# Hybrid diffusion block on one core: fixed order for TensorE alone in gate/up and down, first weights split during the last out-projection tile, down weights loaded in fours

## The chip, the cores and the metric

The kernel runs on one core of a Trainium2 chip. The metric is device time in microseconds of one execution. Of the kernel before, three runs are at hand, 3139.68 to 3141.82 us with a median of 3141.06, and one profiled execution.

## The reference

One transformer-like layer over 2048 latent tokens of width 1024, with a context of 256 tokens. Two head groups (gated linear attention and differential attention) read the same modulated input; this study is about what follows them:

```
mix = concatenate([gla_merge(...), diff_merge(...)], axis=-1) @ w_out[l]
x = x + gt1 * mix
x = x + gt2 * swiglu(modulate(x, norm2_g[l], sh2, sc2), w_ffn_in[l], w_ffn_out[l])

def swiglu(h, w_in, w_out):
    gate, up = jnp.split(h @ w_in, 2, axis=-1)
    return (jax.nn.silu(gate) * up) @ w_out
```

The hidden width is 2816, all arrays are float32.

## The kernel before

Each float32 operand is split into a high and a low part (`split`, L89: a copy to the rounded type on ScalarE at L90, the difference on VectorE at L87), and each product is three matmuls (`mm3`, L93 to L96: high by high, high by low, low by high).

**Order.** Under `tc.manual_schedule(engines=...)` the engines named keep the order in which the kernel writes their instructions. The other engines' order is set when the program is built: a planner goes by modelled times, and of the instructions that it holds ready on an engine it takes the one written first. On the chip every engine runs its instructions in the order so planned. `MS` (L41) names TensorE alone; `MS5` (L42) names TensorE, VectorE (DVE) and ScalarE (ACT). SyncE's DMA queue is never named. The attention and out-projection stages use `MS`, gate/up and down use `MS5` (L1215, L1271).

**Out projection (L910 to L1079).** 16 token tiles from 15 down to 0. `prep` (L971) gates and normalises a tile's mixed heads and transposes them; `main` (L1008) multiplies by the eight split blocks of `w_out` (two column halves, eight row blocks, 48 matmuls), and adds into `x1`. The raw `w_out` blocks are loaded at L932 during and after the attention, into buffers of later tokens (`s4x0`, `s4x1`), of the norm (`s4n`) and of the split mix (`s4h`). For each pair of tiles but the last, `mod2` (L1023) squares (L1029), scales (L1031, on ScalarE), transposes (L1044) and modulates (L1047) them, and either stores the result to DRAM (`h2_d`, L1050) or leaves it in `hb`, four blocks of 4 x 512 tokens (tags hb00 to hb11), for the half of the tokens that comes first in gate/up. `early_ops` prepares two of the seven block operands, slots 0 and 1.

**Gate/up (L1082 to L1249).** A seven-product scheme (after Strassen) for 2 x 2 blocks: gate and up as columns, two halves of the 1024 input rows. A round `n` is one block `j` of 128 hidden columns for one half of the tokens; there are 22 rounds per half, 44 in all. Each round has seven products `i` of twelve matmuls, weights against the token operand `slots[i]` (tiles o0h, o0l to o6h, o6l; 128x2048). `rebuild(hb, i)` (L1092) makes slot `i` from the blocks, with a block sum for i = 1, 4, 5; it runs in round 0 for slots 2 to 6 and in round 21, behind each product, for all slots of the other token half. `fetch` (L1134) loads a round's raw weights (tile wi, two DMAs of 512 KB), `weights(n, i)` (L1141) splits the i-th weight combination into a pair of buffers (wh, wl; seven pairs), with three sums at i = 1 and one at i = 6. It is written `AHEAD` = 3 products before its product. Round 22 uses the weights of round 21 again. `finish` (L1184) evicts each product: e on VectorE (L1195 and others, by the helper's L84) or ScalarE (L1187, L1191, L1202). A later product of a round adds into a bank that `finish` of an earlier one must have read. `last_group` (L1104) normalises tiles 0 and 1 in round 1: loads, ScalarE squares, scaling on VectorE (L1115), transposes (L1122).

**Down (L1251 to L1306).** 16 pairs of token tiles (8 pairs for each half of the 1024 output columns). A pair takes 22 hidden blocks x 2 tiles x 3 = 132 matmuls. `down_weights(dd, j)` (L1259) loads one raw block (128x512, 256 KB, tile wo, three buffers), and splits it into wot. `tokens` (L1209) loads and splits half a tile's activations (tile ar, 704 KB). In pair 0 all 22 blocks are loaded and split; those of the second column half follow in pairs 5 and 7. The pools of this stage open when those of gate/up have closed.

Of the kernel before, what the change touches and what calls it, by code (L numbers as in the profile page):

```python
# [11 lines left out]
F32 = mybir.dt.float32  # L12
# [7 lines left out]
P = 128  # L20
# [15 lines left out]
AHEAD = 3  # L36
# [5 lines left out]
MS5 = {mybir.EngineType.PE, mybir.EngineType.DVE, mybir.EngineType.Activation}  # L42
# [10 lines left out]
def dit_block(ctx: ExitStack, tc: tile.TileContext, x, c, cx, c_ctx, w_mod, b_mod, norm1_g, w_in, gate_up,  # L53
# [32 lines left out]
    def sub(o, a, b, eng=None):  # L86
        (eng or V).tensor_tensor(out=o, in0=a, in1=b, op=ALU.subtract)  # L87

    def split(hi, lo, src):  # L89
        S.activation(hi, src, AF.Copy)  # L90
        sub(lo, src, f(hi))
# [804 lines left out]
    with ExitStack() as st:  # L896
        h2p = st.enter_context(tc.tile_pool(name="s45h", bufs=1, reuse_waits="tile"))
        pad = st.enter_context(tc.tile_pool(name="s45pad", bufs=1, side="right"))
        G.memset(pad.tile([P, 56], F32, name="pad"), 0.0)
        rsk = st.enter_context(ExitStack())  # L900
        st6 = st.enter_context(ExitStack())
        sl0 = st6.enter_context(tc.tile_pool(name="s45o", bufs=1, reuse_waits="tile"))
# [4 lines left out]
        def slot(pool, i):  # L907
            return [pool.tile([P, 4, 512], F32R, name=f"o{i}{u}", tag=f"o{i}{u}") for u in "hl"]

        hb = h2_blocks()  # L910
        slots = {i: slot(sl0, i) for i in range(2)}
        st1 = st.enter_context(ExitStack())
        xp = [st1.enter_context(tc.tile_pool(name=f"s4x{u}", bufs=2, side="right", reuse_waits="tile")) for u in range(2)]
        xnp = st1.enter_context(tc.tile_pool(name="s4n", bufs=2, side="right", reuse_waits="tile"))
# [4 lines left out]
        pp = st1.enter_context(tc.tile_pool(name="s4p", bufs=2, reuse_waits="tile"))  # L919
        gl = st1.enter_context(tc.tile_pool(name="s4g", bufs=2, reuse_waits="tile"))  # L920
        wk = st1.enter_context(tc.tile_pool(name="s4k", bufs=2, reuse_waits="tile"))
        ps_gm = st1.enter_context(tc.tile_pool(name="s4gm", bufs=1, space=PSUM, reuse_waits="tile"))
        ps_tp = st1.enter_context(tc.tile_pool(name="s4tp", bufs=3, space=PSUM, reuse_waits="tile"))
        ps_mm = st1.enter_context(tc.tile_pool(name="s4mm", bufs=4, space=PSUM, reuse_waits="tile"))
        gt1 = gp.tile([P, D], F32, name="gt1")
# [3 lines left out]
        for n, k in enumerate(ORD0):  # L929
            pool, tag = {3: (xnp, "xn"), 2: (xnp, "xn"), 1: (ph, "mh"), 0: (ph, "ml")}.get(k, (xp[k // 2 % 2], "xt"))  # L930
            w = pool.tile([P, D], F32, name="wr", tag=tag)
            load(w, w_out[0, k * P:(k + 1) * P, :])  # L932
            with tc.high_priority(offset=tc.cur_priority - marks[3 + 2 * n]):
                split(*wo[k], w)

        def gla_out(lt, mixt):
# [22 lines left out]
            sq = gl.tile([P, 4, P], F32, name="at", tag="at", bufs=1)  # L959
# [11 lines left out]
        def prep(lt):  # L971
# [3 lines left out]
            xt = xp[lt // 2 % 2].tile([P, D], F32, name="xt", tag="xt")  # L975
# [47 lines left out]
        def mod2(g):  # L1023
            b, o0 = (g % 4) // 2, (g % 2) * 256
            xn = []
            for t in range(2):
# [4 lines left out]
                S.activation(n_t, x1s[2 * g + t], AF.Copy, scale=rs)  # L1031
# [30 lines left out]
        x1s = {}  # L1062
        with tc.manual_schedule(engines=MS):
            for _ in prep(NT - 1):
                pass
            for lt in reversed(range(NT)):
                seq = {}
                if lt:
                    p_ = prep(lt - 1)
                    for n in PREP:  # L1070
                        seq.setdefault(n, []).append(p_)
                if lt % 2 and lt + 1 < NT:
                    m_ = mod2((lt + 1) // 2)
                    for n in MOD:
                        seq.setdefault(n, []).append(m_)
                for n, _ in enumerate(main(lt)):
                    for q_ in seq.get(n, ()):
                        next(q_, None)
        st1.close()  # L1079


        SEQ_P = ((0, True), (1, True), (0, False), (2, True), (3, True), (2, False), (3, False))  # L1082
        sl1 = st6.enter_context(tc.tile_pool(name="s5o", bufs=1, reuse_waits="tile"))
        rwp = rsk.enter_context(tc.tile_pool(name="s5r", bufs=2, side="right", reuse_waits="tile"))
        opp = st6.enter_context(tc.tile_pool(name="s5w", bufs=7, side="right", reuse_waits="tile"))
        tmp = st6.enter_context(tc.tile_pool(name="s5t", bufs=1, side="right", reuse_waits="tile"))
        ep = st6.enter_context(tc.tile_pool(name="s5e", bufs=1, side="right", reuse_waits="tile"))
        ps5 = st6.enter_context(tc.tile_pool(name="s5ps", bufs=2, space=PSUM, reuse_waits="tile"))

        slots[6] = slot(sl1, 6)  # L1090

        def rebuild(blocks, i, fresh):  # L1092
# [9 lines left out]
            split(*slots[i], (b11, b11, b21, b12, b12, b21, b22)[i])  # L1102
# [31 lines left out]
        def fetch(n):  # L1134
            j = work[n][1]
            w = rwp.tile([P, KT, 2, P], F32, name="wi", tag="wi")
# [4 lines left out]
        def weights(n, i):  # L1141
# [16 lines left out]
            kept[n, i] = [opp.tile([P, 4, P], F32R, name=f"w{u}", tag=f"w{u}") for u in "hl"]  # L1158
# [54 lines left out]

        flat = [(n, i) for n in range(len(work)) for i in range(7)]
        with tc.manual_schedule(engines=MS5):  # L1215
            with tc.high_priority(offset=100):
                fetch(0)
                for m in range(AHEAD):
                    weights(*flat[m])
            fetch(1)  # L1220
            late = last_group()
            for m, (n, i) in enumerate(flat):
                if n == 0 and i < 5:
                    rebuild(hb, i + 2, i != 4)
                if m + AHEAD < len(flat):
                    weights(*flat[m + AHEAD])
# [15 lines left out]
                if n == len(work) - 1 and i in (0, 4):  # L1242
                    t = i // 4
# [102 lines left out]
```

## Time and profile before

| | us |
|---|---|
| median of 3 runs | 3141.06 |
| profiled execution | 3141.57 |
| span of its trace | 3139.8 |
| out projection, from its first transposes to its last matmul | 1521.78 to 1757.93 |
| gate/up | 1757.93 to 2644.46 |
| down | 2644.46 to 3139.80 |

The span goes from the first to the last instruction of the trace; the profiled execution's own time is 1.8 us more. Times of the trace count from the span's start. A line such as L90 is one of the kernel's, often a helper's, so an instruction is told by its tiles: "wl<-wi,wh" is the low half of a gate/up weight. Matmuls of 512 columns are shown with 0.39 us or more and overlap; the distance between their starts is what each one costs. What stands behind "<-" in brackets is the instruction that ended the engine's idle time.

### The profile page before, as it was taken

To read this page: it belongs to the slowest core of one execution; us is meant where nothing else is said; L and a number is where in the kernel's file an instruction comes from. 1 tells how busy PE (TensorE), PEld (TensorE's weight loads), DVE (VectorE), ACT (ScalarE), POOL (GpSimd) and SP (SyncE) were. 2 spreads that over 40 slices of the span, in tenths; PEclk is the share of its full clock that TensorE was granted. 3 is DMA by queue.
4 is the path that set the end of the run, shared out by engine and by line. 5 is a ranking of instruction groups with operands and counts; after the bars stand their busy time and mean duration, and the time that the engine had idled before them with its cause. 6 is when DMAs were issued, how large, how long until landed. Compare 5 with 4: busy or idle time off the path is not lost.

```text
span 3139.8 us, 41871 instructions
## 1 busy us (share of the span) xinstructions
PE 3033.0 (97%) x15124; PEld 2492.8 (79%) x15124; DVE 2197.4 (70%) x4774; ACT 1422.0 (45%) x2273; POOL 463.8 (15%) x290
## 2 busy tenths in 40 slices
PE   7999999999989999999999799999899999999999
PEld 4888889888867777777777688888688887888887
DVE  7878677878889999999777666666666665334332
ACT  5333456666657777777554423232322233213121
POOL 2111100000046665554111000000000000000000
PEclk9999999999999999999999899999899999999999
DMA  8866511121241312220545342222222224544432
GB/s 308 290 238 218 172 69 65 63 90 66 62 142 43 83 49 77 50 60 28 168 168 174 108 131 84 81 83 78 61 81 81 81 84 144 168 147 166 151 132 89
DMA packets 319553, 363.47 MB, mean 116 GB/s; under 512 B 25841, under 2 KB 256690, under 8 KB 312690
## 3 DMA queue, kind: packets, MB, share of 16 engines
q1 hardware_dynamic: 316754, 351.36, 35.4%
q0 software_dynamic: 2304, 8.39, 0.7%
q8 instruction: 120, 1.97, 0.3%
q10 hardware_dynamic: 288, 1.05, 0.1%
q14 instruction: 87, 0.71, 0.1%
HBM read 249.96 MB, written 110.76 MB: 115 GB/s over the span
## 4 chain that ended last, share of the span: by engine, by line
PE 64%; DVE 3%; ACT 2%; DMA 1%; issue 1%; POOL 0%; SPq 0%; DVEq 0%; ACTq 0%; POOLq 0%
PE p L94 8%; PE p L95 8%; PE p L96 8%; PE o L95 6%; PE o L96 6%; PE o L94 6%; PE s L777 4%; PE s L778 4%; PE t L822 4%; PE o L845 3%; PE mm L94 2%; PE mm L96 2%; PE mm L95 2%; DMA wo<-in_w_ffn_out 1%; POOL p L84 0%
## 5 line engine op out<-in xcount | busy, mean ns | idle before, releaser
L84 POOL TENSOR_TENSOR p<-p,p 128x1152 f32<-128x1152 f32 x124 | 354.9, 2883 | 283.3 <-DVE p L809 175.8
L779 DVE TENSOR_SCALAR_CACHE_REDUCE p<-s 128x512 f32<-128x512 f32 (+1 forms) x640 | 381.8, 630 | 13.1 <-PE s L778 9.0
L94 PE MATMUL mm<-wh,hh 128*128 128x512 f32 (+2 forms) x976 | 379.0, 388 | 0.0
L96 PE MATMUL mm<-wh,hl 128*128 128x512 f32 (+2 forms) x976 | 355.1, 364 | 0.0
L95 PE MATMUL mm<-wl,hh 128*128 128x512 f32 (+2 forms) x976 | 354.0, 363 | 0.0
L785 ACT ACTIVATE p<-p,nm 128x2304 f32<-128x2304 f32 x128 | 283.8, 2217 | 44.5 <-DVE nm L783 44.5
L777 PE MATMUL s<-k,qh 128*128 128x512 f32 (+1 forms) x640 | 276.4, 436 | 7.1 <-DVE p L779 6.3
L95 PE MATMUL o<-wot,ah 128*128 128x512 f32 x682 | 266.3, 390 | 1.5 <-DVE wot L87 1.5
L94 PE MATMUL o<-wot,ah 128*128 128x512 f32 x682 | 265.9, 390 | 0.9 <-ACT wot L90 0.9
L96 PE MATMUL o<-wot,al 128*128 128x512 f32 x682 | 266.2, 390 | 0.5 <-DVE al L87 0.5
L84 DVE TENSOR_TENSOR e<-p,e 128x512 f32<-128x512 f32 x220 | 151.4, 688 | 137.7 <-PE p L96 137.7
L778 PE MATMUL s<-k,ql 128*128 128x512 f32 (+1 forms) x640 | 236.0, 375 | 1.5 <-DMA ql<-ql 1.5
L90 ACT ACTIVATE ah<-ar 128x1408 fp32r<-128x1408 f32 x62 | 82.5, 1374 | 309.9 <-PE o L95 293.8
L90 ACT ACTIVATE wh<-s 128x512 fp32r<-128x512 f32 x129 | 80.5, 624 | 291.6 <-DVE s L87 291.6
L96 PEld LDWEIGHTS mm<-wh,hl 128*128 128x128 f32 x976 | 184.9, 189 | 29.8
L94 PEld LDWEIGHTS mm<-wh,hh 128*128 128x128 f32 x976 | 186.1, 191 | 23.0 <-issue 0.7
L95 PEld LDWEIGHTS mm<-wl,hh 128*128 128x128 f32 x976 | 186.4, 191 | 21.5 <-issue 0.5
L87 DVE TENSOR_TENSOR al<-ar,ah 128x1408 fp32r<-128x1408 f32 x62 | 98.2, 1621 | 129.5 <-ACT ah L90 129.5
L822 PE MATMUL t<-ident,p 128*128 128x128 f32 x1152 | 173.2, 272 | 0.9 <-POOL p L84 0.8
L87 DVE TENSOR_TENSOR wl<-s,wh 128x512 fp32r<-128x512 f32 x129 | 88.9, 690 | 115.1 <-ACT wh L90 115.1
L822 PEld LDWEIGHTS t<-ident,p 128*128 128x128 f32 x1152 | 141.4, 141 | 35.3 <-issue 3.9
L777 PEld LDWEIGHTS s<-k,qh 128*128 128x128 f32 x640 | 122.4, 191 | 57.6 <-DVE p L779 15.7
(308 smaller groups left out, 7183.5 us busy)
## 6 DMA issues: line engine op xcount, KB each, us to landing
ar<-act SPq DMA_DIRECT2D x64, 704.0 KB, 4.7
wi<-in_w_ffn_in SPq DMA_DIRECT2D x86, 512.0 KB, 4.5
act<-e SPq DMA_DIRECT2D x88, 256.0 KB, 2.6
wm<-in_w_mod SPq DMA_DIRECT2D x32, 512.0 KB, 4.8
xt<-in_x SPq DMA_DIRECT2D x30, 512.0 KB, 4.0
wr<-in_w_in SPq DMA_DIRECT2D x12, 1024.0 KB, 7.5
wo<-in_w_ffn_out SPq DMA_DIRECT2D x44, 256.0 KB, 3.5
hdh<-hh SPq DMA_DIRECT2D x9, 1024.0 KB, 4.8
```

Of the source, the lines that this page charges most:

```text
L84: (eng or V).tensor_tensor(out=o, in0=a, in1=b, op=ALU.add)
L87: (eng or V).tensor_tensor(out=o, in0=a, in1=b, op=ALU.subtract)
L90: S.activation(hi, src, AF.Copy)
L94: T.matmul(ps, a[0], b[0], start=start, stop=False, **how)
L95: T.matmul(ps, a[0], b[1], start=False, stop=False, **how)
L96: T.matmul(ps, a[1], b[0], start=False, stop=stop, **how)
L777: T.matmul(ps[:, 0:n], qd[0][c_][:, qc], ks_[h, c_][:, o0:o0 + n], start=True, stop=False)
L778: T.matmul(ps[:, 0:n], qd[1][c_][:, qc], ks_[h, c_][:, o0:o0 + n], start=False, stop=True)
L779: V.tensor_scalar(out=pr[c_][:, o0:o0 + n], in0=ps[:, 0:n], scalar1=1.0, scalar2=-3.0e38, op0=ALU.mult, op1=ALU.max, accum_out=mx[:, j:j + 1])
L785: S.activation(pr[c_], pr[c_], AF.Exp, bias=nm, accum_out=l)
L822: T.transpose(pt[:, i, :], as_[bi][i][:, kt * P:(kt + 1) * P], ident)
L845: T.matmul(po[:, 0:nq, :], v[0], at[0], start=kt == 0, stop=kt == NKT - 1)
```

## The change

- Gate/up and down name TensorE alone (`MS` for `MS5`), so VectorE's and ScalarE's instructions are placed by the planner. A few are pinned with `keep_in_program_order`: such an instruction is issued behind the one written just before it on its engine.
- In `mod2` the scaling goes from ScalarE to VectorE.
- Tile 0 of the out projection gets a token buffer of its own (`s4xl`), and the token buffers, norm buffers and some others close before it. In their place, six weight-buffer pairs (seven before) and two raw buffers of one tile each are opened, and during `main(0)` the first six weight combinations of round 0 are split (`EARLY` = 6). The last weight of round 21, which must outlive a round, goes to a free raw buffer.
- Block splits 2 and 3 are written before round 0's loop, the rest at products 2 to 4.
- `down_weights` takes several blocks: fours for the first column half, twos for the second. Raw blocks go to o0h and o1h, four split ones to o0l and o1l. The first eight blocks are loaded in round 43, and tile 8's first tokens are loaded in round 41.
- The down stage's `x1t` and `ot` tiles use the tags hb00 to hb11; `x1t` is loaded before the second half of a pair.

```diff
-AHEAD = 3
+AHEAD, EARLY = 3, 6
...
-MS5 = {mybir.EngineType.PE, mybir.EngineType.DVE, mybir.EngineType.Activation}
...
+        sl0 = st.enter_context(tc.tile_pool(name="s45o", bufs=1, reuse_waits="tile"))
...
+        xlp = rsk.enter_context(tc.tile_pool(name="s4xl", bufs=1, side="right", reuse_waits="tile"))
...
+        st1e = st1.enter_context(ExitStack())
+        xp = st1e.enter_context(tc.tile_pool(name="s4x", bufs=4, side="right", reuse_waits="tile"))
+        xnp = st1e.enter_context(tc.tile_pool(name="s4n", bufs=2, side="right", reuse_waits="tile"))
...
-                S.activation(n_t, x1s[2 * g + t], AF.Copy, scale=rs)
+                V.tensor_scalar(out=n_t, in0=x1s[2 * g + t], scalar1=rs, scalar2=None, op0=ALU.mult)
...
-                sub(s3, a11, a21)
+                d = sub(s3, a11, a21)
+                if n == 1:
+                    tc.keep_in_program_order(d)
...
+            if n == NH - 1 and i == 6:
+                w = rwp[NH % 2].tile([P, KT, 2, P], F32R, name="wi", tag="wi")
+                kept[n, i] = w[:, 0:2].rearrange("p a b n -> p (a b) n"), w[:, 2:4].rearrange("p a b n -> p (a b) n")
...
+        def down_weights(dd, js):
+            b, m = js[0] // len(js) % 2, len(js)
+            w = sl0.tile([P, m, 512], F32, name="wo", tag=f"o{b}h")
+            load(w, w_fo[0, js[0] * P:(js[0] + m) * P, dd * 512:(dd + 1) * 512].rearrange("(j p) n -> p j n", p=P))
+            if dd == 0 and js[0] == 0 or dd == 1 and js[0] in (2, 4):
+                for z in range(0, m, 2):
+                    v = (z if dd == 0 else js[0] - 2) // 2
+                    wt = sl0.tile([P, 2, 2, 512], F32R, name="wot", tag=f"o{v}l")
+                    for q in range(2):
+                        split(wt[:, q, 0], wt[:, q, 1], w[:, z + q])
+                        downs[dd, js[z + q]] = wt[:, q, 0], wt[:, q, 1]
+            else:
+                waiting.extend((dd, j, w[:, z]) for z, j in enumerate(js))
+
+        def place_weights():
+            for dd, j, w in waiting:
+                wt = wop.tile([P, 2, 512], F32R, name="wot", tag="wot")
+                split(wt[:, 0], wt[:, 1], w)
+                downs[dd, j] = wt[:, 0], wt[:, 1]
+            waiting.clear()
...
+            st1e.close()
+
+            opp = st6.enter_context(tc.tile_pool(name="s5w", bufs=6, side="right", reuse_waits="tile"))
+            rwp = [st6.enter_context(tc.tile_pool(name=f"s5r{u}", bufs=1, side="right", reuse_waits="tile")) for u in range(2)]
+            tmp = st6.enter_context(tc.tile_pool(name="s5t", bufs=1, side="right", reuse_waits="tile"))
+            fetch(0)
+            for n, _ in enumerate(main(0)):
+                if n % 2 == 0 and n // 2 < EARLY:
+                    weights(0, n // 2)
...
-        with tc.manual_schedule(engines=MS5):
-            with tc.high_priority(offset=100):
-                fetch(0)
-                for m in range(AHEAD):
-                    weights(*flat[m])
+        with tc.manual_schedule(engines=MS):
             fetch(1)
+
+            for i in (2, 3):
+                for ins in rebuild(hb, i, True):
+                    tc.keep_in_program_order(ins)
             late = last_group()
             for m, (n, i) in enumerate(flat):
-                if n == 0 and i < 5:
-                    rebuild(hb, i + 2, i != 4)
-                if m + AHEAD < len(flat):
+                if n == 0 and 1 < i < 5:
+                    rebuild(hb, i + 2, True)
+                if EARLY <= m + AHEAD < len(flat):
                     weights(*flat[m + AHEAD])
...
+                if n == len(work) - 3 and i == 0:
+                    tokens(8, 0, h2p.tile([P, HC, P], F32, name="ar", tag="hb10"), first_pair(0))
+                if n == len(work) - 1:
+                    if i in (1, 2):
+                        down_weights(0, range(4 * i - 4, 4 * i))
...
-        with tc.manual_schedule(engines=MS5):
+        with tc.manual_schedule(engines=MS):
...
-                        for j in range(HC, NH):
-                            down_weights(0, j)
+                        for j in range(8, NH, 4):
+                            down_weights(0, range(j, min(j + 4, NH)))
+                            place_weights()
```

## Rows read from the trace of the kernel before

**Rows 1.** the page's busy times: us, share of the span, instructions
```profile
PE 3033.0 (97%) x15124; PEld 2492.8 (79%) x15124; DVE 2197.4 (70%) x4774; ACT 1422.0 (45%) x2273; POOL 463.8 (15%) x290
```

**Rows 2.** busy time by stretch: length, engines (instructions), granted clock, DMA share, GB/s
```profile
1521.78:1757.93 236.15, 221.97 (x1124) 183.80 (x1125) 163.22 (x334) 105.04 (x302) 28.19 (x30) 0.98 0.48 159
1745.00:1757.93 12.93, 12.93 (x62) 10.74 (x61) 4.55 (x8) 1.23 (x2) 0.53 (x1) 1.00 0.53 165
1757.93:1824.00 66.07, 50.36 (x185) 38.27 (x184) 47.23 (x59) 27.01 (x34) 0.53 (x1) 0.85 0.43 143
1824.00:2185.76 361.76, 361.76 (x1597) 299.55 (x1596) 224.72 (x344) 106.06 (x190) 0.00 (x0) 1.00 0.29 86
2185.76:2244.62 58.86, 43.22 (x169) 34.67 (x168) 38.55 (x36) 20.22 (x20) 0.00 (x0) 0.86 0.12 36
2244.62:2644.46 399.84, 399.84 (x1765) 330.89 (x1763) 246.23 (x376) 118.24 (x209) 0.00 (x0) 1.00 0.30 90
2644.46:2686.14 41.68, 36.27 (x138) 27.58 (x137) 22.41 (x29) 19.06 (x27) 0.00 (x0) 0.92 0.60 189
```

**Rows 3.** TensorE's waits: releaser, us in total, times, longest; two stretches
```profile
PE tp L1044 <- ACT xn L1031: 10.8, 7, 1.7
...
PE p L94 <- DVE e L84: 11.9, 2, 7.2
PE p L94 <- ACT e L1187: 8.4, 1, 8.4
PE p L1122 <- DVE lxn L1115: 4.9, 2, 4.5
```

**Rows 4.** timeline, out projection and last group: start, us, instruction, wait before it
```profile
1679.47 0.28 ACT L142 ACTIVATE n_sd<-ss,eps_t 128x1 f32<-128x1 f32 x1
1680.64 1.15 ACT L1031 ACTIVATE xn<-xt,n_rs 128x1024 f32<-128x1024 f32 x1 [0.32 <-DVE n_rs L144]
...
1681.84 0.55 PE L1044 MATMUL tp<-ident,xn 128*128 128x128 f32 x3 [1.52 <-ACT xn L1031]
...
1802.81 1.42 DVE L1115 TENSOR_SCALAR lxn<-lx,l_rs 128x1024 f32<-128x1024 f32 x2
```

**Rows 5.** timeline around the first seam, queue of SyncE and three engines
```profile
1748.20 15.65 SPq L1138 DMA_DIRECT2D wi<-in_w_ffn_in  x4
...
1752.88 0.63 ACT L90 ACTIVATE wh<-wi 128x512 fp32r<-128x512 f32 x1 [6.88 <-DMA wi<-in_w_ffn_in]
...
1759.48 0.68 DVE L87 TENSOR_TENSOR wl<-wi,wh 128x512 fp32r<-128x512 f32 x1
1775.71 2.29 DVE L87 TENSOR_TENSOR o4l<-hb,o4h 128x2048 fp32r<-128x2048 f32 x1 [1.98 <-ACT o4h L90]
...
1808.92 0.60 PE L1122 MATMUL p<-ident,lxn 128*128 128x128 f32 x4
1809.27 0.48 PE L94 MATMUL p<-o2h,wh 128*128 128x512 f32 x1
```

**Rows 6.** timeline at the second seam, ScalarE and TensorE
```profile
2225.56 1.89 ACT L90 ACTIVATE o6h<-hb 128x2048 fp32r<-128x2048 f32 x1
...
2227.99 0.80 PE L94 MATMUL p<-o2h,wh 128*128 128x512 f32 x1 [8.42 <-ACT e L1187]
2228.59 0.63 PE L95 MATMUL p<-o2l,wh 128*128 128x512 f32 x1
2229.01 0.63 PE L96 MATMUL p<-o2h,wl 128*128 128x512 f32 x1
```

**Rows 7.** third seam's ScalarE splits (busy, idle before); DMA issues with us to landing
```profile
L90 ACT ACTIVATE wot<-wo 128x512 fp32r<-128x512 f32 x22 | 13.5, 628 | 19.7 <-DMA wo<-in_w_ffn_out 19.3
...
wo<-in_w_ffn_out SPq DMA_DIRECT2D x44, 256.0 KB, 3.5
wr<-in_w_in SPq DMA_DIRECT2D x12, 1024.0 KB, 7.5
```

**Rows 8.** timeline of SyncE's queue at the end of the attention
```profile
1488.58 0.81 SPq L932 DMA_DIRECT2D wr<-in_w_out  x2
```

More of the change, by code (lines that the diff above doesn't have):

```diff
@@ new lines, in place_weights @@
+        def place_weights():
[4 more added lines that the diff above has]
+            waiting.clear()
+        x1s = {}
+        with tc.manual_schedule(engines=MS):
+            for _ in prep(NT - 1):
+                pass
+            for lt in reversed(range(1, NT)):
+                seq = {}
+                p_ = prep(lt - 1)
+                for n in PREP:
+                    seq.setdefault(n, []).append(p_)
+                if lt % 2 and lt + 1 < NT:
+                    m_ = mod2((lt + 1) // 2)
+                    for n in MOD:
+                        seq.setdefault(n, []).append(m_)
+                for n, _ in enumerate(main(lt)):
+                    for q_ in seq.get(n, ()):
+                        next(q_, None)
+            st1e.close()
[6 more added lines that the diff above has]
+                    weights(0, n // 2)
@@ L1220, in dit_block @@
+        st1.close()
+        sl1 = st6.enter_context(tc.tile_pool(name="s5o", bufs=1, reuse_waits="tile"))
+        ep = st6.enter_context(tc.tile_pool(name="s5e", bufs=1, side="right", reuse_waits="tile"))
+        ps5 = st6.enter_context(tc.tile_pool(name="s5ps", bufs=2, space=PSUM, reuse_waits="tile"))
+        first[6, "h"] = sl1.tile([P, 4, 512], F32R, name="o6h", tag="o6h")
+        flat = [(n, i) for n in range(len(work)) for i in range(7)]
+        with tc.manual_schedule(engines=MS):
             fetch(1)
+            for i in (2, 3):
+                for ins in rebuild(hb, i, True):
+                    tc.keep_in_program_order(ins)
@@ L1241, in dit_block @@
                     fetch(n + 2)
-                if n == len(work) - 1 and i in (0, 4):
-                    t = i // 4
-                    ar = rwp.tile([P, KT * 2 * P], F32, name="ar", tag="wi")
-                    tokens(8 + t, 0, ar[:, 0:HC * P].rearrange("p (j t) -> p j t", t=P),
-                           [h2p.tile([P, 2048], F32R, name=f"c{t}{u}", tag=f"hb{t}{u}")[:, 0:HC * P]
-                            .rearrange("p (j t) -> p j t", t=P) for u in range(2)])
+                if n == len(work) - 3 and i == 0:
[3 more added lines that the diff above has]
+                        down_weights(0, range(4 * i - 4, 4 * i))
+                    if i == 4:
+                        ar = rwp[0].tile([P, KT * 2 * P], F32, name="ar", tag="wi")
+                        tokens(9, 0, ar[:, 0:HC * P].rearrange("p (j t) -> p j t", t=P), first_pair(1))
         st6.close()
@@ L1270, in dit_block @@
         pairs = [(dd, lt) for dd in range(2) for lt in (*range(8, 16, 2), *range(0, 8, 2))]
-        with tc.manual_schedule(engines=MS5):
+        with tc.manual_schedule(engines=MS):
             for n, (dd, lt) in enumerate(pairs):
                 js = slice(dd * 512, (dd + 1) * 512)
-                ps, x1t = [], []
+                ps = [ps6.tile([P, 512], F32, name="o", tag="o") for _ in range(2)]
+                x1t = []
                 for c_ in range(2):
```

92 lines of the change are left out of this document (30 added, 62 removed).

## The prediction

> **What bounds the kernel now.** I read the busy shares first [rows 1]: TensorE is busy for 97% of the span, so a change that leaves the matmuls as they are can win only what TensorE loses in waits, and at half clock after them. The table by stretches says where that is [rows 2]. From 1824.00 to 2185.76 stand 19 rounds of gate/up without a gap: 361.76/19 = 19.04 us a round of 84 matmuls, 0.2267 us each, at granted clock 1.00. The 21 rounds from 2244.62 cost the same. VectorE, at 224.72/19 = 11.8 us a round, has 7 us to spare there. The losses sit at the seams:
>
> - First seam, 1757.93 to 1824.00: two rounds (38.08 us) and 16 transposes (fours of 1809.27 - 1808.92 = 0.35 us [rows 5], 1.4 us in all) take 66.07 us, a loss of 26.6 us. VectorE is busy for 47.23 of the 66.
> - Second seam, 2185.76 to 2244.62, where the token blocks are rebuilt for the other half of the tokens: two rounds in 58.86 us, a loss of 20.8.
> - Third seam, 2644.46 to 2686.14, the start of the down projection: 138 matmuls (31.3 us) in 41.68, a loss of 10.4.
> - In the out projection TensorE waits seven times for the scaled tokens (L1031), 10.8 us [rows 3].
>
> That is 68.6 us in reach. The list of waits names the releasers [rows 3]: an eviction on VectorE (11.9 us), one on ScalarE (8.4), the last group's scaling (4.9). None is long work itself. An eviction takes 0.69 us, but it stands in written order behind block splits of 2.29 us, and those wait for ScalarE: "o4l" sat 1.98 us for its high half while other work was queued behind it [rows 5]; at the second seam the 8.42 us wait ends only once ScalarE has done the 1.89 us of o6h ahead of the eviction [rows 6]. After a long wait matmuls start 0.43 us apart (2228.59, 2229.01) in place of 0.2267, at the lower of the two clock levels, 1.2 GHz [rows 6]; the granted clock of the seams is 0.85, 0.86 and 0.92 [rows 2].
>
> **The change, part by part.** The sums are against the profiled execution, 3141.57 us; the median of the three runs is 0.5 us less.
>
> *Scaling moved to VectorE (out projection).* Two ScalarE instructions of 1.15 us become VectorE ones of 1.42/2 = 0.71 us [rows 4], in each of seven groups (10 us more of VectorE, which has 236.15 - 163.22 = 73 us free there [rows 2]). The second token's square root (1679.47) no longer stands behind the first one's scaling: 1.04 us earlier; its scaling is 0.44 us shorter and loses the 0.32 us hop. That is 1.8 us against a wait of 1.52. Two gating products and an eviction of 0.69 us may stand ahead on VectorE, so I take 1.2 of each 1.52: **-8.4 us** (bounds 0 and -10.8).
>
> *First round's weights in the last out-projection tile.* Now the raw weights are asked for behind the four stores of that queue (1748.20) and split from 1752.88; the low half waits until 1759.48, behind the last addition [rows 5]. The change writes six splits with their three sums into that tile: nine VectorE instructions of 0.69 us (6.2 us) and six of 0.63 on ScalarE. VectorE is busy for 4.55 of the 12.93 us there [rows 2], so they are hidden if the load comes a few us sooner: its buffer is freed by the last token's gating, long before the four stores. That it comes no sooner is a rival.
>
> *Free order on VectorE and ScalarE, first seam.* What must precede the seventh product (due at 1757.93 + 6 x 2.72 = 1774.2) on VectorE: five low halves and two block sums, 7 x 2.29 = 16.0; three evictions and the seventh weight's subtraction and split, 5 x 0.69 = 3.4. From 1759.5 (the last addition, ahead of which two of the block splits are pinned not to go) that ends at 1779, a hop of 0.9 us to ScalarE included near 1779.8: 5.6 us late. In the second round the last group's scaling stands behind the backlog, some 3 us late, and ten matmuls at half clock lose 10 x 0.2 = 2. So 11 us stay: **-15.6**. Bounds: VectorE's work alone (47.23 - 6.2 = 41.0 against 39.5 of TensorE) leaves 1.5, a gain of 25; if only the moved splits count, the gain is 6.2.
>
> *Second seam.* VectorE must do ten block operations (22.9 us) and fifteen small ones (10.3) between the first product's end (2188.5) and the last one of the next round (due 2221.1): 33.2 us in 32.6, so it only just fits. In the free order small ones no longer wait behind a stuck split, but the fourth product's eviction still comes after o0l, a sum, o2l and o1l: 4.3 us late, and twelve matmuls at half clock add 2.4. I leave 7: **-13.8** (bounds: 1 left, or 14 left).
>
> *Third seam.* 44 loads of 256 KB become 17: six for the first column half, eleven of 512 KB for the second. Eight rows' weights (2 MB) come during the last gate/up round, into o0h and o1h, dead after its first two products; one token load moves two rounds earlier. ScalarE's 22 splits there waited 19.3 us for such loads [rows 7]. The rest comes in pieces of 1 MB, two buffers; a 1 MB load lands in 7.5 us [rows 7], four rows are used up in 4 x 6 x 0.2267 = 5.4. The pieces for rows 16 and 20 share a buffer, so the last one is asked for near 2666 and just meets its use at 2671.6. 3.7 MB of weights, 2.9 of tokens and 0.5 of others in 30 us are 237 GB/s, against 189 now [rows 2]. I leave 2.4: **-8.0** (bounds -10.4 and 0). The Trainium skill (DMA: Bandwidth & Descriptors, section "Anatomy of one DMA") gives 2.0 us plus bytes/436e3: an estimate of 4.4 us for 1 MB; by it this seam would leave nothing and the sum would be 2.4 us lower. The measured 7.5 stands.
>
> *Buffers.* The token buffer set apart pushes one norm buffer under the last attention buffer, so one more raw out-projection weight (512 KB) is loaded near 1488.6, beside the two that already are [rows 8]. The first product that it feeds starts after 1521.78 [rows 2]; I take 0, and as bound 7.5 us, the landing of a load twice its size [rows 7]. Six weight buffers for seven, with three products of lead, hold nothing back: a buffer is asked for three products after its last use. Later token loads for x1 sit in dead blocks, loaded half a token pair (66 matmuls, 15 us) ahead of need, twice what the 1 MB load takes: 0. The end of the kernel is untouched.
>
> Sum: 8.4 + 15.6 + 13.8 + 8.0 = 45.8; 3141.57 - 45.8 = 3095.8, in terms of the median **3095 us**.
>
> **The rivals.**
>
> *The order packs badly (20%).* VectorE is near its limit at both first seams, so its work could set the time: the poor bounds there (6.2 and 6.8) and half of the other two terms (4.2 and 4.0) make 21.2, giving 3120. For it: 47.23 us of 66 and 33.2 against 32.6. Against it: VectorE sat 1.98 us at a time in the seams, which the free order fills.
>
> *It doesn't do what it says at the ends (12%).* If the first weights land no sooner and the 1 MB pieces late, the splits come after 1757.93 and the third seam keeps its loss: 45.8 - 6.2 - 8.0 = 31.6, giving 3109. For it: the four stores ahead in the queue [rows 5].
>
> *Every wait goes (8%).* The four lower bounds, 10.8 + 25 + 19.8 + 10.4 = 66, giving 3075.
>
> *Slower: the freed queues stall in the steady rounds (9%).* The order is planned at build time from modelled durations and run in that order; if a weight split is planned ahead of an eviction and its raw data or high half is late on the chip, the eviction waits behind it, TensorE behind that, and every one of 40 rounds pays. The Trainium skill (TensorE: Matmul & The Clock Gate, section on the array's architecture, "Engine queue depths") says that VectorE and ScalarE queues are strictly first in, first out; by that the freedom ends at build time. The trace agrees: "o4l" held back what was ready behind it for 1.98 us [rows 5]. It decides from 45.8/40 = 1.15 us a round; at 2 us a round it is +80 - 45.8, giving 3175. Against it: 7 us of VectorE slack in each round, and the out projection, which has run in planned order all along, has TensorE busy for 94% [rows 2].
>
> *Nothing moves (3%).* Gains and such stalls cancel: 3141.
>
> **How the numbers follow.** My forecast has 48%, with 3080 to 3107 as its own range. Two tenths of a per cent (6.3 us) is what a measurement of this kernel can tell from no change. The forecast, the packing, the ends and the full gain are all faster: 0.88, of which bad packing gives 0.01 to "same": 0.87, 0.04 and, for the stalls, 0.09. The range runs from the full gain, 3075, to beyond bad packing, 3122.
>
> **What would show it.** Right: splits of the first weights between 1746 and 1758 and TensorE starting the second product without a wait; one wait of 2 to 4 us in each of the first two seams where there were two to five; first down-projection matmul right behind the last gate/up one; no wait of transposes for L1031. Rounds of 19.04 us must stay. Wrong: any wait in the steady rounds; VectorE idle while TensorE waits at a seam; a wait for down weights past 2660 (counted in the old times); the clock of the seams staying near 0.85.

## The result and the profile after

The changed kernel takes 3094.45 us (median of 4 runs, 3092.13 to 3094.64), the kernel before 3141.44 us on the same chip (4 runs, 3139.68 to 3147.43): a ratio of 0.9845, with a 95% interval of 0.9828 to 0.9862. The forecast was 3095. The profiled execution of the changed kernel took 3094.64 us, its span is 3092.9 us.

The busy times of the changed kernel, from the page (us, share, instructions), against [rows 1]. PE is TensorE's matmuls, PEld its weight loads, DVE VectorE, ACT ScalarE and POOL GpSimd:

```profile
PE 3016.1 (98%) x15124; PEld 2483.7 (80%) x15124; DVE 2203.8 (71%) x4788; ACT 1423.5 (46%) x2259; POOL 463.8 (15%) x290
```

The number of matmuls is the same; TensorE's 17 us less of busy time fit the higher granted clock of the seams (0.93, 1.00 and 1.00 for 0.85, 0.86 and 0.92), that is, fewer matmuls at half clock. The table by stretches (same columns as [rows 2]), cut at the same places of the program: out projection, first seam, 19 steady rounds, second seam, 21 steady rounds, start of the down projection, rest:

```profile
1522.04:1751.02 228.98, 221.21 (x1125) 183.14 (x1125) 174.15 (x355) 96.91 (x295) 28.35 (x30) 0.98 0.51 166
1751.02:1800.74 49.72, 42.95 (x186) 34.48 (x184) 45.96 (x59) 22.31 (x29) 0.53 (x1) 0.93 0.52 179
1800.74:2162.50 361.76, 361.76 (x1598) 299.55 (x1596) 227.12 (x342) 115.11 (x191) 0.00 (x0) 1.00 0.28 82
2162.50:2204.86 42.36, 38.93 (x170) 31.22 (x168) 38.54 (x36) 21.65 (x21) 0.00 (x0) 1.00 0.22 67
2204.86:2604.70 399.84, 399.84 (x1766) 331.08 (x1764) 247.25 (x374) 126.44 (x209) 0.00 (x0) 1.00 0.31 90
2604.70:2645.00 40.30, 37.39 (x161) 29.87 (x160) 25.63 (x32) 19.34 (x27) 0.00 (x0) 1.00 0.78 262
2645.00:3092.90 447.90, 442.62 (x1953) 366.18 (x1951) 138.39 (x137) 85.63 (x76) 0.00 (x0) 1.00 0.41 135
```

The steady rounds are what they were, to a hundredth of a microsecond each. The out projection is 7.2 us shorter, the first seam 66.07 - 49.72 = 16.35, the second 58.86 - 42.36 = 16.5. The down part, from the end of the steady rounds, took 3139.8 - 2644.46 = 495.3 and takes 488.2: 7.1 less. Together 47.2, less 0.26 by which the out projection started later: the 46.9 us between the two spans.

TensorE's waits from 1500 us on (but for two ahead of transposes of the mixed heads, 4.1 and 4.2 us, before 4.0 and 3.4, and one of 0.2; releaser, us in total, times, longest), against [rows 3]:

```profile
PE p L93 <- DVE o4l L86: 5.4, 1, 5.4
PE tp L1046 <- DVE xn L1033: 3.6, 7, 0.9
PE p L92 <- DVE e L83: 3.4, 2, 2.3
PE o L93 <- DVE wot L86: 1.5, 2, 1.3
PE o L92 <- ACT wot L89: 1.4, 2, 1.1
PE p L92 <- ACT o4h L89: 1.4, 1, 1.4
```

The largest wait of gate/up was 8.4 us for an eviction behind ScalarE's split; now it is 5.4, for a block itself. The timeline of the first seam (start, us, instruction, wait before it) shows why that one is left:

```profile
1756.60 2.29 DVE L86 TENSOR_TENSOR o3l<-hb,o3h 128x2048 fp32r<-128x2048 f32 x1
1758.80 0.69 DVE L83 TENSOR_TENSOR e<-p,e 128x512 f32<-128x512 f32 x1
1759.40 4.49 DVE L86 TENSOR_TENSOR hb<-hb,hb 128x2048 f32<-128x2048 f32 x2
1763.80 0.69 DVE L86 TENSOR_TENSOR wl<-s,wh 128x512 fp32r<-128x512 f32 x1
1764.40 0.69 DVE L83 TENSOR_TENSOR e<-p,e 128x512 f32<-128x512 f32 x1
1765.00 2.28 DVE L86 TENSOR_TENSOR o6l<-hb,o6h 128x2048 fp32r<-128x2048 f32 x1
1767.20 2.29 DVE L86 TENSOR_TENSOR o4l<-hb,o4h 128x2048 fp32r<-128x2048 f32 x1
...
1761.72 1.91 ACT L89 ACTIVATE o4h<-hb 128x2048 fp32r<-128x2048 f32 x1 [1.53 <-DVE hb L86]
...
1769.54 0.80 PE L93 MATMUL p<-o4l,wh 128*128 128x512 f32 x1 [5.36 <-DVE o4l L86]
1770.13 0.63 PE L94 MATMUL p<-o4h,wl 128*128 128x512 f32 x1
1770.56 0.63 PE L92 MATMUL p<-o4h,wh 128*128 128x512 f32 x1
```

VectorE never rests there, but o6l, which is needed two products later, runs ahead of o4l, for which TensorE sits idle; o4h was there at 1763.63 (1761.72 + 1.91). The matmuls behind that wait start 0.43 us apart, at 1.2 GHz; the granted clock of the whole seam is 0.93.

At the second and third seams these are all of TensorE's waits:

```profile
2178.61 0.50 PE L92 MATMUL p<-o5h,wh 128*128 128x512 f32 x1 [2.35 <-DVE e L83]
2199.28 0.50 PE L92 MATMUL p<-o5h,wh 128*128 128x512 f32 x1 [1.09 <-DVE e L83]
...
2610.59 0.49 PE L92 MATMUL o<-wot,c 128*128 128x512 f32 x1 [0.29 <-ACT wot L89]
2612.34 0.50 PE L93 MATMUL o<-wot,c 128*128 128x512 f32 x1 [1.25 <-DVE wot L86]
2635.31 0.50 PE L92 MATMUL o<-wot,ah 128*128 128x512 f32 x1 [1.14 <-ACT wot L89]
2636.04 0.50 PE L93 MATMUL o<-wot,ah 128*128 128x512 f32 x1 [0.23 <-DVE wot L86]
```

### The profile page after: what moved, and what is told of

Read it like the earlier page. It is cut to its first block, busy times and chain, and to the rows that moved or that the text cites. A ratio compares the mean times of both kernels' runs of the same rounds, so it can differ in the third digit from the quotient of the medians.

```text
span 3092.9 us, 41887 instructions
## 1 busy us (share of the span) xinstructions
PE 3016.1 (98%) x15124; PEld 2483.7 (80%) x15124; DVE 2203.8 (71%) x4788; ACT 1423.5 (46%) x2259; POOL 463.8 (15%) x290
## 4 chain that ended last, share of the span: by engine, by line
PE 63%; DVE 4%; issue 2%; DMA 1%; ACT 1%; POOL 1%; DVEq 0%; SPq 0%; ACTq 0%; POOLq 0%
PE p L93 9%; PE p L92 9%; PE p L94 9%; PE o L93 6%; PE o L94 6%; PE o L92 6%; PE s L775 4%; PE s L776 4%; PE t L820 4%; PE o L843 3%; PE mm L92 1%; PE mm L93 1%; PE mm L94 1%; POOL p L83 0%; DMA wo<-in_w_ffn_out 0%
## 5 line engine op out<-in xcount | busy, mean ns | idle before, releaser
L89 ACT ACTIVATE wh<-wi 128x512 fp32r<-128x512 f32 x172 | 108.4, 631 | 293.4 <-PE p L93 228.4
```

The lines of the kernel that those rows point to most:

```text
L89: return S.activation(hi, src, AF.Copy), sub(lo, src, f(hi))
```

## Experiments

The main theory: small evictions and late blocks stood on VectorE behind long splits that waited for ScalarE or were not yet wanted. The free order took that away; the moved weights add room at the first seam, and the early loads at the third. The rival: the moved work did it, and the order is worth little. No run undoes by itself the pins, the early writing of blocks 2 and 3, the earlier token loads or the new places of the down stage's buffers.

The stages ahead of the out projection differ by a few us between executions, though the kernels hardly differ there (the out projection starts at 1519.62 to 1525.94). So beside the medians stands what each trace shows from the first gate/up product on. "First seam" is the time of the first two rounds, "second seam" that of rounds 22 and 23, counted from one (n = 21 and 22 in the kernel), "to the end" the time from the first gate/up product to the end of the span, all read off the timeline.

| kernel | median, us | first product at | first seam | second seam | to the end |
|---|---|---|---|---|---|
| before | 3141.44 | 1757.93 | 66.07 | 58.86 | 1381.9 |
| changed | 3094.45 | 1751.02 | 49.72 | 42.36 | 1341.9 |
| scaling on ScalarE | 3100.00 | 1758.36 | 47.61 | 43.15 | 1340.6 |
| fixed order in gate/up | 3122.84 | 1749.93 | 60.12 | 57.71 | 1372.8 |
| before, order freed | 3120.06 | 1761.41 | 54.77 | 41.53 | 1356.8 |
| first weights late | 3099.85 | 1751.21 | 54.84 | 42.44 | 1346.9 |
| fixed order in down | 3092.86 | 1750.92 | 49.96 | 42.44 | 1339.6 |
| single-row loads | 3096.64 | 1755.27 | 49.76 | 42.58 | 1342.1 |
| no early rows | 3102.61 | 1748.76 | 49.34 | 43.05 | 1351.3 |
| o6l behind o5l | 3092.94 | 1749.69 | 48.33 | 43.00 | 1341.0 |
| sum on GpSimd | 3099.48 | 1750.65 | 50.14 | 46.21 | 1345.5 |
| order by need | 3091.37 | 1752.94 | 46.82 | 42.42 | 1339.2 |
| one more place | 3091.24 | 1750.42 | 46.98 | 41.33 | 1336.9 |

The steady rounds are 19.04 us in all of them. One caution for the last two columns: matmuls at half clock follow some waits in one kernel and not in another (below, at "o6l behind o5l"), which is worth some 1.4 us each time, so differences of that size are not yet the work of an edit.

**The scaling alone undone.**

```
-                V.tensor_scalar(out=n_t, in0=x1s[2 * g + t], scalar1=rs, ...)
+                S.activation(n_t, x1s[2 * g + t], AF.Copy, scale=rs)
```

> The changed kernel with the scaling of the normalized tokens back on ScalarE (one line). Theory (short scaling on an engine with room, no square root behind it): TensorE's seven waits before the transposes of L1046 come back, 3.6 us in all becomes about 10.8, so +7 us on the changed kernel, near 3101.6. Rival (what fell there came from the other buffers or the new plan of the whole stage, not from this line): the waits stay near 3.6 us and the time within 2 us of 3094.5.

3100.00 us (ratio to before 0.9863, 0.9849 to 0.9878). The waits of this kernel:

```profile
PE tp L1046 <- ACT xn L1033: 10.8, 7, 1.7
```

They are back to the tenth. The first gate/up product comes 7.3 us later, 0.8 of them because the out projection started that much later (1522.84). The time rose by 5.6, not 7: the first seam became 2.1 us shorter, as VectorE went on while TensorE waited ahead of it (o2l starts 1.8 us behind the first product, in the changed kernel 3.4).

**The free order alone undone, in gate/up.**

```
-        with tc.manual_schedule(engines=MS):
+        with tc.manual_schedule(engines=MS5):
             fetch(1)
```

> The changed kernel with VectorE and ScalarE again in written order in gate/up only; the early weights, the loads in fours and the scaling stay. Theory (the small evictions stood behind long splits, the free order took them out): the second seam goes from 42.4 us back to 54 to 59 and the first from 49.7 to about 59, so some +23 us, near 3117. Rival (the moved work did it, the order little): both seams within 3 us of the changed kernel's, time up by 5 us at most.

3122.84 us (0.9936, 0.9919 to 0.9952): 28 us lost, more than expected. The first two seams are as the theory has them, and the two large waits at the second one are those of the kernel before [rows 3], to a tenth:

```profile
2192.79 0.77 PE L93 MATMUL p<-o5h,wh 128*128 128x512 f32 x1 [7.22 <-DVE e L84]
2214.31 0.79 PE L93 MATMUL p<-o2h,wh 128*128 128x512 f32 x1 [8.37 <-ACT e L1169]
```

What the expectation lacked is the third seam: the early down weights are split in gate/up, so there, too, the order was fixed, and the first down product came 3.7 us late (2633.09 for 2610.32 + 19.04): in the last gate/up round TensorE waits 1.8 us for an eviction. The down projection's own waits grow by 1.5 us.

**The free order alone, in the kernel before.**

```
-        with tc.manual_schedule(engines=MS5):
+        with tc.manual_schedule(engines=MS):
```

(at both places.)

> The kernel before, with nothing but the free order of VectorE and ScalarE in gate/up and down. Theory: the second seam needs nothing else, 58.9 us becomes 43 to 46; the first gains about 9 of its 66.1, the third nothing; 22 to 25 us in all, near 3117. Rival (free order without the moved work makes splits stand before evictions in other places): the first seam is as long as before or longer, and less than 16 us are won in all. A second rival (stalls in the steady rounds): more than 19.04 us in a steady round, time above 3141.

3120.06 us (0.9927, 0.9912 to 0.9942), 23 us won, as the theory said: by the trace 17.3 at the second seam and 7.8 up to the end of the first (the third round starts at 1816.18, before at 1824.00). At the third, where the theory had nothing, 3.5 us are lost: from the end of the steady rounds it takes 498.9 us for 495.3. Its waits name what the moved work is for:

```profile
PE o L94 <- ACT wot L90: 9.5, 1, 9.5
PE p L94 <- ACT wh L90: 7.4, 1, 7.4
PE p L1172 <- DVE wl L87: 3.4, 1, 3.4
PE p L1172 <- ACT wh L90: 3.3, 1, 3.3
```

Three of them are the first round's weights, whose load comes late here and whose splits the planner put behind the blocks; the 9.5 us are the down weights, whose first splits on ScalarE the planner put behind a token split that waited for its load.

**The first weights held back.** The six splits and their sums are bound behind the last addition of the out projection on VectorE (`lv`):

```
+            lv = next(i for i in reversed(nc.cur_bb.bb.instructions) if i.engine == mybir.EngineType.DVE)
+            with tc.issue_after(lv):
+                for m in range(AHEAD):
+                    weights(*flat[m])
...
```

> The changed kernel with VectorE's part of the first round's weights (splits and sums) held behind the last addition of the out projection; the load comes as early as in the changed kernel and the order stays free. Theory (VectorE's backlog sets the first seam): nine instructions of 0.6 us more behind that addition, the seam goes from 49.7 us to about 56, time +6, near 3100.5. Rival (the free order hides them, as VectorE waits in between anyway): seam and time within 2 us of the changed kernel's.

3099.85 us (0.9866, 0.9851 to 0.9880): 5.4 us, seam 54.84. VectorE is busy for 50.52 of those 54.84 us, 4.6 more than in the changed kernel's 49.72. So at this seam the order was worth 10.4 (fixed order) and the moved splits 5.1. Part of these 5.1 is order again: held back, a sum for the second product's weights stands behind o6l on VectorE (it starts at 1757.01), and TensorE waits for the high half made from it:

```profile
1758.42 0.79 PE L92 MATMUL p<-o1h,wh 128*128 128x512 f32 x1 [3.74 <-ACT wh L89]
```

**Fixed order in the down projection only** (MS5 at the second place, as above).

> The changed kernel with VectorE and ScalarE in written order in the down projection only; gate/up stays free and the early loads stay. Theory (the third seam was a matter of loads, not of order): the down projection's waits for weights go up by less than 2 us, time within 2 us of 3094.5. Rival (the free order is what lets the first down weights be split beside the last gate/up products): TensorE waits 5 us or more longer at the start of the down projection, time 3099 or more.

3092.86 us (0.9843, 0.9830 to 0.9856): nothing lost. By the trace, from the end of the steady rounds the written order is even 2.6 us shorter (485.6 for 488.2), as TensorE's waits for down weights fall from 2.9 to 0.8 us; no matmul is at half clock there in either. ScalarE's timeline shows what the planned order did there (first the changed kernel, then this one):

```profile
2608.64 1.38 ACT L89 ACTIVATE ah<-ar 128x1408 fp32r<-128x1408 f32 x1 [2.39 <-DMA ar<-act]
2609.93 2.17 ACT L89 ACTIVATE wot<-wo 128x512 fp32r<-128x512 f32 x4
...
2606.39 2.18 ACT L90 ACTIVATE wot<-wo 128x512 fp32r<-128x512 f32 x4
```

In the changed kernel ScalarE sits idle for a token load with four splits of down weights behind it, which in written order run at once. So the free order is no gain in this stage; that it costs something there is shown by the trace alone, as the intervals of the medians overlap.

**Loads of down weights cut into single rows.**

```
-            load(w, w_fo[0, js[0] * P:(js[0] + m) * P, ...].rearrange("(j p) n -> p j n", p=P))
+            for z in range(m): load(w[:, z], w_fo[0, (js[0] + z) * P:(js[0] + z + 1) * P, ...])
```

> The changed kernel with each load of two or four rows of down weights cut into loads of one row (256 KB) into the same buffers, at the same places. Theory (the third seam was won by asking for eight rows a round early, not by the size of a load): the time stays within 2 us of the changed kernel's 3094.5, and TensorE's waits for down weights (2.9 us in all) change by less than 2 us. Rival (fewer and larger loads are what counts): those waits grow by 4 us or more, time 3098.5 or more.

3096.64 us (0.9857, 0.9844 to 0.9871), 2.2 us above the changed kernel's, just over the theory's 2. In the profiled execution the out projection already started 3.9 us later than the changed kernel's (1525.94); from the first product on it took 1342.1 for 1341.9, and the waits at the third seam went from 2.9 to 1.6 us: the one at the last rows is gone. What that saves is lost again at half clock, as seven matmuls behind the wait that is left start 0.43 us apart (from 2618.24), where the changed kernel's stayed 0.23 apart behind the same wait. Larger loads are not what won the seam.

**The early rows undone.** Both loads of eight rows come behind the last store of gate/up on SP's queue (`ls`):

```
-                    if i in (1, 2):
-                        down_weights(0, range(4 * i - 4, 4 * i))
...
+                        with tc.issue_after(ls):
+                            for j in (0, 4):
+                                down_weights(0, range(j, j + 4))
```

> The changed kernel with the first eight rows of down weights (2 MB, two loads) asked for only behind the last store of gate/up, in place of one round before the end. Theory: the loss of the third seam comes back, and more, since a load of 1 MB lands later than one of 256 KB did: TensorE waits 8 to 14 us at the first down weights, time 3102 to 3108. Rival (the early rows are hidden anyway, the order of ScalarE's splits set the old loss): less than 3 us.

3102.61 us (0.9878, 0.9864 to 0.9891). One wait takes back the third seam's gain and more:

```profile
2613.83 0.79 PE L92 MATMUL o<-wot,c 128*128 128x512 f32 x1 [10.92 <-ACT wot L89]
```

This undoes more than the change did. The kernel before, too, asked for its first three rows well before the end of gate/up (2644.46); ScalarE split them only behind the last eviction:

```profile
2628.94 0.57 SPq L1261 DMA_DIRECT2D wo<-in_w_ffn_out  x1
2632.32 0.86 SPq L1261 DMA_DIRECT2D wo<-in_w_ffn_out  x2
...
2645.92 1.65 ACT L90 ACTIVATE wot<-wo 128x512 fp32r<-128x512 f32 x3
```

In the changed kernel three loads, twelve rows, are asked for before the end of gate/up (2604.70), as the third piece, written in the down projection, moved ahead, too:

```profile
2588.57 9.02 SPq L1203 DMA_DIRECT2D wo<-in_w_ffn_out  x3
```

New are thus nine more rows before that end, and the first four splits before it (at 2594.03). So the run shows that rows must be asked for before the end; which of the two won the seam, no run tells apart.

**o6l behind o5l**, by an edge of the same kind on VectorE at the first seam.

> The changed kernel with the low half of the seventh block (o6l) bound to come behind that of the sixth (o5l) on VectorE, at the first seam only. In the changed kernel o6l ran for 2.2 us ahead of o4l, which TensorE waited 5.4 us for. Theory (the order chosen there was bad): o4l is ready 2.2 us sooner less 0.6 for a weight split that moves ahead of it, the first two rounds go from 49.7 to 47 to 48 us, time 3092 to 3093. Rival (VectorE's sum of work sets the seam, any order gives the same, and the last group's scaling now comes too late): within 1 us or slower.

3092.94 us (0.9846, 0.9833 to 0.9860), which the runs can't tell from the changed kernel. The trace shows the seam at 48.33, the wait for o4l at 3.8 us in place of 5.4; from the first product on, 0.9 us are left of it, as the second seam took 0.6 us more. That is the clock: behind the same wait of 2.35 us, ahead of the same matmul, eight matmuls start some 0.43 us apart here (1.6 us lost, granted clock of the seam 0.96), where in the changed kernel none did (1.00):

```profile
2175.89 0.50 PE L92 MATMUL p<-o5h,wh 128*128 128x512 f32 x1 [2.35 <-DVE e L83]
...
2176.50 0.63 PE L94 MATMUL p<-o5h,wl 128*128 128x512 f32 x1
2176.92 0.63 PE L92 MATMUL p<-o5h,wh 128*128 128x512 f32 x1
```

**The sum for the sixth product on GpSimd**, with the order o4l, o5l, o6l:

```
-                sub(b21, b21, b11)
+                sub(b21, b21, b11, G)
```

> As the run before (o4l, o5l, o6l in this order at the first seam), and the block difference for the sixth product (128x2048) computed by GpSimd, which has nothing to do there, in place of VectorE, at both seams. Theory (VectorE's backlog sets both seams): 2.2 us less of VectorE ahead of the late pieces in each; first two rounds 49.7 to about 45, rounds 22 and 23 from 42.4 to about 40.5, time near 3088. Rival (GpSimd needs some 4.6 us for such a tile, as a subtraction of 128x2048 does in the set-up, and VectorE slows down beside it or waits for it): no gain on the run before, or a loss.

3099.48 us (0.9868, 0.9855 to 0.9882): the theory fell and the rival came. The timeline of GpSimd and VectorE at the first seam:

```profile
1755.61 6.57 POOL L86 TENSOR_TENSOR hb<-hb,hb 128x2048 f32<-128x2048 f32 x1 [1.46 <-DVE o2l L86]
...
1755.44 2.29 DVE L86 TENSOR_TENSOR o3l<-hb,o3h 128x2048 fp32r<-128x2048 f32 x1
1757.64 0.68 DVE L83 TENSOR_TENSOR e<-p,e 128x512 f32<-128x512 f32 x1
1758.24 6.09 DVE L86 TENSOR_TENSOR hb<-hb,hb 128x2048 f32<-128x2048 f32 x1
1764.25 0.68 DVE L86 TENSOR_TENSOR wl<-s,wh 128x512 fp32r<-128x512 f32 x1
```

VectorE's difference of two blocks, 2.2 us elsewhere, took 6.09: it ended 2.15 us after GpSimd did (1762.18), so it ran only then; and GpSimd's own 6.57 us include some 2.1 in which o3l, begun just before it, ran to its end (1757.73). The eviction at 1757.64, one of whose inputs is in PSUM, wasn't held. At the second seam o3l took 6.05 us in the same way. The Trainium skill (SBUF — State Buffer, section "SBUF: two separate sides") says that a VectorE instruction with two SBUF inputs and a GpSimd instruction that reads SBUF exclude each other for their whole length. By that rule work moved to GpSimd is no relief for such instructions; the trace agrees, with 6.09 for 2.2.

**The order by need.** Beside o6l, two weight splits behind o5l; at the second seam o1l behind the fourth product's eviction (the rebuild written two products later); the token split of the down projection held to the last rounds; single-row loads.

```
-                    rebuild(hb0, i, True)
+                    e_ = next(q for q in reversed(nc.cur_bb.bb.instructions) if q.engine == mybir.EngineType.DVE)
+                    for k in {1: (), 3: (1, 3)}.get(i, (i,)):
+                        rebuild(hb0, k, True, e_ if k == 1 else None)
...
```

> The changed kernel with five places of VectorE's order bound by what TensorE needs next, and single-row loads of the down weights: o6l behind o5l, and two weight splits that nobody waits for behind o5l, too (first seam); o1l behind the eviction of the fourth product, and the token split that is first used in the down projection held to the last rounds (second seam). Theory (what is left at the seams are splits ahead of their turn): first seam 48.3 with the first of these alone, 47 with all; second seam 42.4 less the 2.3 us wait for that eviction and 1.1 for the one behind the token split, 39 to 40; third seam 1.4 us less; from the first gate/up product to the end 1341.9 becomes 1335 to 1337, time 3087 to 3090. Rival (VectorE's sum of work sets the seams, so a wait that goes comes back behind the next piece): 1340 or more, time 3092 or more.

3091.37 us (0.9837, 0.9824 to 0.9851). The first seam did as expected, 46.82; the 1339.2 us to the end lie between theory and rival. The second seam stayed at 42.42: the wait moved one product on. TensorE's waits there fell from 3.4 us (2.35 and 1.09) to 2.0, and half clock behind the one that is left took that back, 1.4 us in seven starts 0.43 us apart (the next expectation counts twelve; of those, the first five are not at half clock):

```profile
2180.42 0.50 PE L92 MATMUL p<-o6h,wi 128*128 128x512 f32 x1 [1.97 <-DVE e L83]
...
2181.77 0.63 PE L94 MATMUL p<-o6h,wi 128*128 128x512 f32 x1
2182.19 0.63 PE L92 MATMUL p<-o6h,wi 128*128 128x512 f32 x1
```

**One more place**: o3l, too, behind an eviction (`4: (3, 4)` in the table above).

> The run before with one more place bound: at the second seam o3l, too, comes behind an eviction (that of the fifth product). In the run before, the wait of 2.35 us behind o1l only became one of 1.97 behind o1l and o3l, one product later, with twelve matmuls 0.43 us apart behind it, and rounds 22 and 23 took 42.4 us as ever. Theory (one more piece ahead of its turn): that wait falls under 0.5 us, rounds 22 and 23 take 39 to 40.5 us, from the first gate/up product to the end 1339.2 becomes 1336 to 1337, time 3088 to 3089. Rival (VectorE has no room at this seam: 33.2 us of work in 32.6): the wait comes back at a later product or at the blocks of the next round, 42 us or more.

3091.24 us (0.9837, 0.9823 to 0.9850), above the theory's 3089. The time to the end is as expected (1336.9), but not for the reason expected: the second seam takes 41.33, as one wait came back a round later, and longer than the 1.97 us that it replaces:

```profile
2194.93 0.47 PE L92 MATMUL p<-o5h,wh 128*128 128x512 f32 x1 [2.47 <-DVE e L83]
```

Of the 2.3 us won on the run before, 1.1 are at this seam and 1.4 in the down projection, which the edit doesn't touch; in both places the run before had seven starts at half clock and this one has none. So no gain of this place itself is shown. By the trace it is 5.0 us shorter than the changed kernel from the first gate/up product on, and neither has half clock behind the first seam. The medians differ by 3.2 us, and the intervals of the ratios overlap, so that it beats the changed kernel is shown by the trace alone; that it beats the kernel before is shown by the runs.

## Why the prediction was right, point by point

**The sum** was 45.8 us and 46.9 came. No term was off by more than 2.7: out projection 8.4 forecast and 7.2 measured, first seam 15.6 and 16.35, second 13.8 and 16.5, third 8.0 and 7.1. That the sum came so near is in part luck: the misses have both signs, and the 16.5 hold some 1.6 us of a clock that stayed up behind a wait after which it fell in the run with o6l behind o5l.

**Buffers.** The forecast had one more raw `w_out` block loaded near 1488.6. In the changed kernel two blocks are loaded at 1466, in place of 906, and two at 1489 as before. The out projection started 0.26 us later; as starts differ by 6.3 us between the traces, the runs can't tell a term of a few us from the 0 forecast.

**Scaling on VectorE.** The mechanism is shown by undoing it. Of each wait of about 1.5 us 0.5 stayed, not 0.3: I took 1.2 off, and 1.03 came (7.2/7).

**First weights in the last tile.** Right, and their worth nearly so: 6.2 was the bound "if only the moved splits count", 5.1 the seam lost without them. The load was asked for at 1731.77, ahead of the four stores, so the rival of the ends fell there. The low halves came late all the same (from 1748.84), but the second product had them without a wait.

**First seam.** The loss left is 10.2 us of the 11 forecast, but not where I put it. I had a late seventh product (5.6), a late scaling of the last group (3) and half clock (2). There is instead the fifth product's block: 1.42 and 5.36 us, some 2.8 of the latter because the planned order runs o6l and a weight split ahead of o4l (with that order bound it is 2.55); half clock costs 4.72 - 11 x 0.2267 = 2.2 (eleven matmuls from 1769.54 to 1774.26); the scaling made no wait. So the step "what must precede the seventh product" took the right backlog (it ended 20.7 us behind the first product, forecast 21.1) and the wrong order, and that the loss left agrees is luck in part. That the order is a cause, and not VectorE's sum of work alone, is shown by the last two runs: bound by need, the same work takes 46.9 us.

**Second seam.** The place was right (the fourth product's eviction behind o2l and o1l), its size too high: 2.35 us for the 4.3 forecast, and no matmuls at half clock where I had 2.4. The 1.09 in the next round, behind a token split, I had not seen. That the order alone won this seam is shown from both sides: 57.71 with it fixed, 41.53 with nothing else.

**Third seam.** Waits of 2.9 us for 2.4 forecast: 1.4 at the last piece, which the sum had just meeting its use (it was asked for 23.6 us behind the end of gate/up, not 21.5), and 1.5 at the fifth row, which it did not have. These 1.5 come from the planned order of ScalarE, and the written order has 0.8. That rows must be asked for before the end of gate/up is shown by undoing it (10.9 us), and that the size of the loads did not win the seam by the single rows. My price for a 1 MB load, 7.5 us, was too high: the five here landed in 5.4 (median).

The estimate of 4.4 us from the Trainium skill (DMA: Bandwidth & Descriptors, "Anatomy of one DMA") was nearer than my row, and a fifth too low. That section gives its figure for a DMA issued by GpSimd, and these loads are issued by SyncE.

**The rivals.** "The order packs badly" was half true: at the first seam (o6l and weight splits ahead of their turn) for about 3 us, and in the down projection for 2.6. The stalls in steady rounds did not come: 19.04 us everywhere, with VectorE's order free.

**The signs.** Those named for "right" came for the first weights, the first down product and the steady rounds. The others came in part: the first seam has two waits (1.4 and 5.4 us) and the second two (2.35 and 1.09), and the transposes still wait 3.6 us in all for the scaling. Two signs of "wrong" came as well, in the third seam alone: the wait at 2635.31 is one for down weights past 2660 in the old times (2675), and VectorE is idle in it, as its next work waits for the same load.

## What to carry to other kernels

Read for each wait what stood ahead of the releaser in its engine's queue: where a 0.7 us eviction stands behind 2.3 us splits that nobody wants yet, order is worth more than speed, and it is won by binding the few instructions that run ahead of their turn. Once an order is free, the line where work is written says little: hold it with an edge to undo it, and read the planned order before the time. Free it stage by stage: here it won 15 us at one seam and lost some 2.6 us in the down projection. Work that is the same can be timed to a microsecond on the trace from a common point on, where whole runs of several milliseconds can't.

## What was not expected of the hardware

- An idle GpSimd was no spare room: its 128x2048 difference took 6.57 us and held VectorE's for 6.09 (2.2 alone).
- Half clock does not follow from the length of a wait alone: 2.35 us at 2178.61 left the matmuls 0.23 us apart; the same wait ahead of the same matmul, in the run with o6l behind o5l, and one of 1.97 us in the order by need were followed by matmuls 0.43 apart. No run here shows what decides it.
- Loads of 256 KB landed in 4.6 us (median of 44) when asked for in a row, loads of 1 MB in 5.4 (median of 5): four times the size for 0.8 us more. Size is not all, as the twelve loads of 512 KB in the changed kernel took 6.3 us (median).
